# Rotating 96 images: 32 KB load runs, 8 KB store runs and half as many transposes for the middle 64

## The chip, the cores and the metric

The kernel runs on 1 core of one Trainium2 chip. The metric is the device time of one execution in microseconds; lower is better. All runs told of here are fast (granted clock 1.0). "Span" is the part of an execution that the profile covers, from its first to its last instruction. The time is 1.8 us longer than the span in most kernels here, and that difference will matter.

## The reference

```python
def setup_inputs():
    batch, c, h, w = 32, 3, 256, 256
    return {"x": np.random.randn(batch, c, h, w).astype(np.float32)}

def reference(x):
    return np.rot90(x, k=1, axes=(-2, -1)).astype(np.float32)
```

There are 96 images of 256 x 256 float32, 25.17 MB in and 25.17 MB out. No arithmetic is done: every byte is loaded once, moved within the core, and stored once.

## The kernel before

Groups of 16 images (4 MB) pass through an input tile S and an output tile U of 32 KB a partition, three buffers each. The kernel relies on VectorE's transpose to swap partitions and elements within blocks of 32 x 32; the access patterns around it do the rest of the rotation. There are two kinds of group. Kind 1 (first and last 16 images) keeps 8 rows of an image in a partition (8 KB runs in DRAM, transfers of 1 MB). Kind 2 (the middle 64 images) keeps 16 rows (16 KB runs, transfers of 2 MB).

```python
KINDS = [1, 2, 2, 2, 2, 1]
# ... (tile pools S and U, 3 buffers each)
for g, kind in enumerate(KINDS):
    # ...
    if kind == 1:
        R = 8
        # ... (views)
        for s in range(4):                       # 4 loads of 1 MB
            eng = nc.scalar if g == 0 and s % 2 else nc.sync
            eng.dma_start(out=Sv[:, s], in_=xv[s])
        for s in range(4):                       # 4 transposes of 128x2048, 4 stores of 1 MB
            # ... (src and dst patterns)
            nc.vector.transpose(dst, src)
            nc.scalar.dma_start(out=ov[s], in_=Uv[:, s])
    else:
        R = 16
        # ... (views)
        for b in range(2):                       # 2 loads of 2 MB
            nc.sync.dma_start(out=Sv[:, b], in_=xv[b])
        src = Sv.rearrange("p b (r k q) -> p q r k b", r=R, q=R)[:, ::-1, :, ::-1]
        dst = Uv.rearrange("p a (q k r) -> p q r k a", q=R, r=R)
        for q in range(R):                       # 16 transposes of 128x512
            nc.vector.transpose(dst[:, q], src[:, q])
        for a in range(2):                       # 2 stores of 2 MB
            nc.scalar.dma_start(out=ov[a], in_=Uv[:, a])
```

Loads are issued from SyncE (queue 1; two of the first four from ScalarE), stores from ScalarE (queue 10).

## Time and profile before

| | before |
|---|---|
| time, median of the first 3 runs | 124.03 us (123.91 to 124.1) |
| span | 122.2 us |
| VectorE busy | 91.5 us, 75% |
| mean DMA rate | 412 GB/s |
| VectorE's program as built | 89 instructions, 72 of them transposes (the trace records 87) |

The page of the kernel before. In the two rows of slices each digit is the busy share of one fortieth of the span in tenths; the GB/s row has the rate of the same slices. Then the DMA queues (packets, MB, share of 16 engines' time), and VectorE's groups of instructions (busy time, mean ns of one, idle time before).

```profile
span 122.2 us, 172 instructions
DVE 91.5 (75%) x72; POOL 0.2 (0%) x4
...
DVE  0039999729999999996599993199999999548000
...
DMA  4999999999999999999999999999999999999993
GB/s 83 418 426 429 445 343 432 464 424 402 426 469 397 429 434 434 429 429 434 429 440 429 429 434 434 424 418 445 418 432 445 402 453 410 464 426 397 426 429 142
DMA packets 4610, 50.34 MB, mean 412 GB/s; under 512 B 513, under 2 KB 513, under 8 KB 513
...
q10 hardware_dynamic: 2592, 27.26, 52.5%
q1 hardware_dynamic: 2016, 23.07, 45.2%
q14 instruction: 2, 0.01, 0.0%
...
L66 DVE STREAM_TRANSPOSE U<-S 128x512 f32<-128x512 f32 x64 | 60.6, 1050 | 9.8 <-DMA S<-in_x_dram 5.5
L50 DVE STREAM_TRANSPOSE U<-S 128x2048 f32<-128x2048 f32 x8 | 31.0, 3950 | 11.3 <-DMA S<-in_x_dram 11.3
```

What to see: the DMA row is 9 from the second slice to the second to last, VectorE's row is not. The DMA engines bound the kernel.

The timeline of the same kernel (start, length, engine, what, how often, and the wait before it). ACTq and SPq are the issues of transfers.

```profile
1.63 45.47 SPq L61 DMA_DIRECT2D S<-in_x_dram  x8
8.17 15.44 DVE L50 STREAM_TRANSPOSE U<-S 128x2048 f32<-128x2048 f32 x4 [8.17 <-DMA S<-in_x_dram]
...
26.77 30.22 DVE L66 STREAM_TRANSPOSE U<-S 128x512 f32<-128x512 f32 x32 [3.16 <-DMA S<-in_x_dram]
...
59.34 15.20 DVE L66 STREAM_TRANSPOSE U<-S 128x512 f32<-128x512 f32 x16 [2.35 <-DMA S<-in_x_dram]
78.88 15.20 DVE L66 STREAM_TRANSPOSE U<-S 128x512 f32<-128x512 f32 x16 [4.33 <-issue]
...
108.69 3.97 DVE L50 STREAM_TRANSPOSE U<-S 128x2048 f32<-128x2048 f32 x1 [3.15 <-DMA S<-in_x_dram]
```

VectorE takes 15.1 to 15.2 us for 16 images and waits before three of the four middle groups, without the DMA row ever falling: its waits cost nothing.

### The profile page before, as it was taken

The numbers are of one execution on the slowest core, as the hardware profiler recorded it, in microseconds if no ns is written. First come the engines' busy times: TensorE is split into PE (matmuls) and PEld (weight loads), VectorE is DVE, ScalarE is ACT, GpSimd is POOL, SyncE is SP. The second block draws the span as 40 slices with busy tenths as digits, with TensorE's granted clock in tenths as the row PEclk, the third lists the DMA queues.
The fourth block names the chain that finished last, engine by engine and source line by source line (L and its number), as shares of the span: only waits on it lengthen the run. The fifth ranks groups of instructions, "written<-read, shape, count | busy, mean of one in ns | idle before, by whom it ended". The sixth has DMA issues, their size and how long they took to land.

```text
span 122.2 us, 172 instructions
## 1 busy us (share of the span) xinstructions
DVE 91.5 (75%) x72; POOL 0.2 (0%) x4
## 2 busy tenths in 40 slices
DVE  0039999729999999996599993199999999548000
POOL 0000000000000000000000000000000000000000
DMA  4999999999999999999999999999999999999993
GB/s 83 418 426 429 445 343 432 464 424 402 426 469 397 429 434 434 429 429 434 429 440 429 429 434 434 424 418 445 418 432 445 402 453 410 464 426 397 426 429 142
DMA packets 4610, 50.34 MB, mean 412 GB/s; under 512 B 513, under 2 KB 513, under 8 KB 513
## 3 DMA queue, kind: packets, MB, share of 16 engines
q10 hardware_dynamic: 2592, 27.26, 52.5%
q1 hardware_dynamic: 2016, 23.07, 45.2%
q14 instruction: 2, 0.01, 0.0%
HBM read 25.17 MB, written 25.17 MB: 412 GB/s over the span
## 4 chain that ended last, share of the span: by engine, by line
DMA 62%; DVE 27%; SPq 1%; issue 1%; DVEq 0%
DMA S<-in_x_dram 46%; DVE U L66 24%; DMA out_dram<-U 16%; DVE U L50 3%; SPq L45 1%; SPq L61 1%; DVEq L66 0%
## 5 line engine op out<-in xcount | busy, mean ns | idle before, releaser
L66 DVE STREAM_TRANSPOSE U<-S 128x512 f32<-128x512 f32 x64 | 60.6, 1050 | 9.8 <-DMA S<-in_x_dram 5.5
L50 DVE STREAM_TRANSPOSE U<-S 128x2048 f32<-128x2048 f32 x8 | 31.0, 3950 | 11.3 <-DMA S<-in_x_dram 11.3
L83 POOL MEMSET const-uint8-127<- 128x1 uint8 x1 | 0.1, 102 | 0.0
L83 POOL MEMSET const-bfloat16-1.0<- 128x1 bf16 x1 | 0.1, 101 | 0.0
L83 POOL MEMSET const-float32-0.0<- 128x1 f32 x1 | 0.1, 98 | 0.2 <-issue 0.2
L83 POOL MEMSET const-float32-1.0<- 128x1 f32 x1 | 0.1, 98 | 0.0
## 6 DMA issues: line engine op xcount, KB each, us to landing
S<-in_x_dram SPq DMA_DIRECT2D x8, 2048.0 KB, 25.0
out_dram<-U ACTq DMA_DIRECT2D x8, 2048.0 KB, 18.0
out_dram<-U ACTq DMA_DIRECT2D x8, 1024.0 KB, 15.0
S<-in_x_dram SPq DMA_DIRECT2D x6, 1024.0 KB, 26.5
S<-in_x_dram ACTq DMA_DIRECT2D x2, 1024.0 KB, 9.9
```

The source lines that it names most:

```text
L45: eng.dma_start(out=Sv[:, s], in_=xv[s])
L50: nc.vector.transpose(dst, src)
L61: nc.sync.dma_start(out=Sv[:, b], in_=xv[b])
L66: nc.vector.transpose(dst[:, q], src[:, q])
L83: nc = _bacc.Bacc("TRN2", target_bir_lowering=False, num_devices=1)
```

## The change

Intent: for the middle 64 images, load in runs of 32 KB (32 rows a partition) with one transfer of 4 MB per 16 images, and store in runs of 8 KB, also in one transfer. The longer load run lets 8 transposes of 128x1024 do what 16 of 128x512 did. S and U become rings of twelve 8 KB slots, so the capacity is the same; the first and last 16 images are treated as before.

```diff
-    KINDS = [1, 2, 2, 2, 2, 1]
+    R = 8
...
+    AS = [1] * 4 + [4] * 4 + [1] * 4
+    NS = NU = 12
...
+    for i, a in enumerate(AS):
+        s = n % NS
...
+        RI = R * a
+        S = S_all[:, s : s + a].rearrange("p a f -> p (a f)")
+        U = U_all[:, s : s + a]
...
-            for b in range(2):
-                nc.sync.dma_start(out=Sv[:, b], in_=xv[b])
+            eng.dma_start(
+                out=S, in_=xg[n : n + a].rearrange("a (qk f) -> qk a f", f=RI * W)
+            )
...
-            src = Sv.rearrange("p b (r k q) -> p q r k b", r=R, q=R)[:, ::-1, :, ::-1]
-            dst = Uv.rearrange("p a (q k r) -> p q r k a", q=R, r=R)
+        src = S.rearrange("p (r k q) -> p q r k", r=RI, q=R)[:, ::-1, :, ::-1]
+        dst = U.rearrange("p a (q k r) -> p q r k a", q=R, r=RI)
...
             for q in range(R):
                 nc.vector.transpose(dst[:, q], src[:, q])
-            for a in range(2):
-                nc.scalar.dma_start(out=ov[a], in_=Uv[:, a])
...
+            nc.scalar.dma_start(
+                out=og[n : n + a].rearrange("a (p f) -> p a f", p=P), in_=U
+            )
```

More of the change, by code (lines that the diff above doesn't have):

```diff
@@ L20 @@
     P = 128
-    G = 16
-    KINDS = [1, 2, 2, 2, 2, 1]
-    assert len(KINDS) * G == N
-    F = G * H * W // P
-    fp32 = mybir.dt.float32
-    xf = x.rearrange("b c h w -> (b c h w)").rearrange("(g f) -> g f", g=N // G)
-    of = out.rearrange("b c h w -> (b c h w)").rearrange("(g f) -> g f", g=N // G)
-    in_pool = ctx.enter_context(tc.tile_pool(name="in_pool", bufs=3))
-    out_pool = ctx.enter_context(tc.tile_pool(name="out_pool", bufs=3))
-    for g, kind in enumerate(KINDS):
-        S = in_pool.tile([P, F], fp32, name="S")
-        U = out_pool.tile([P, F], fp32, name="U")
-        if kind == 1:
-            R = 8
-            Sv = S.rearrange("p (s f) -> p s f", s=4)
-            Uv = U.rearrange("p (s f) -> p s f", s=4)
-            xv = xf[g].rearrange("(s p f) -> s p f", s=4, p=P)
-            ov = of[g].rearrange("(s p f) -> s p f", s=4, p=P)
-            for s in range(4):
-                eng = nc.scalar if g == 0 and s % 2 else nc.sync
-                eng.dma_start(out=Sv[:, s], in_=xv[s])
-            for s in range(4):
-                src = Sv[:, s].rearrange("p (r k q) -> p q r k", r=R, q=R)[:, ::-1, :, ::-1]
-                dst = Uv[:, s].rearrange("p (q k r) -> p q r k", q=R, r=R)
-                nc.vector.transpose(dst, src)
-                nc.scalar.dma_start(out=ov[s], in_=Uv[:, s])
-        else:
-            R = 16
-            Sv = S.rearrange("p (b f) -> p b f", b=2)
-            Uv = U.rearrange("p (a f) -> p a f", a=2)
-            xv = xf[g].rearrange("(b a qk f) -> b qk a f", b=2, a=2, f=F // 2)
-            ov = of[g].rearrange("(b a qk f) -> a qk b f", b=2, a=2, f=F // 2)
-            for b in range(2):
-                nc.sync.dma_start(out=Sv[:, b], in_=xv[b])
-            src = Sv.rearrange("p b (r k q) -> p q r k b", r=R, q=R)[:, ::-1, :, ::-1]
-            dst = Uv.rearrange("p a (q k r) -> p q r k a", q=R, r=R)
@@ new lines @@
+    R = 8
+    F = R * W
+    G = N // 4
+    AS = [1] * 4 + [4] * 4 + [1] * 4
+    assert sum(AS) == G
+    NS = NU = 12
+    fp32 = mybir.dt.float32
+    xf = x.rearrange("b c h w -> (b c h w)")
+    of = out.rearrange("b c h w -> (b c h w)")
+    xg = xf.rearrange("(n f) -> n f", n=G)
+    og = of.rearrange("(n f) -> n f", n=G)
+    S_all = ctx.enter_context(tc.tile_pool(name="S", bufs=1)).tile([P, NS, F], fp32, name="S_all")
+    U_all = ctx.enter_context(tc.tile_pool(name="U", bufs=1)).tile([P, NU, F], fp32, name="U_all")
@@ new lines @@
+    n = 0
+    for i, a in enumerate(AS):
+        s = n % NS
+        assert s + a <= NS
+        RI = R * a
+        S = S_all[:, s : s + a].rearrange("p a f -> p (a f)")
+        U = U_all[:, s : s + a]
+        eng = nc.scalar if i in (1, 3) else nc.sync
+        if a == 1:
+            eng.dma_start(out=S, in_=xg[n].rearrange("(p f) -> p f", p=P))
+        else:
+            eng.dma_start(
[3 more added lines that the diff above has]
+        dst = U.rearrange("p a (q k r) -> p q r k a", q=R, r=RI)
+        if a == 1:
+            nc.vector.transpose(dst[:, :, :, :, 0], src)
+        else:
@@ L65 @@
             for q in range(R):
                 nc.vector.transpose(dst[:, q], src[:, q])
-            for a in range(2):
-                nc.scalar.dma_start(out=ov[a], in_=Uv[:, a])
+        if a == 1:
+            nc.scalar.dma_start(out=og[n].rearrange("(p f) -> p f", p=P), in_=U[:, 0])
+        else:
+            nc.scalar.dma_start(
+                out=og[n : n + a].rearrange("a (p f) -> p a f", p=P), in_=U
+            )
+        n += a
 _INS = ['x']
```

## The prediction

> **What bounds the kernel now.** The 16 DMA engines. The page's slices show them over 90% busy from the second slice to the second to last, at about 430 GB/s; 50.3 MB move. In the packet records the first data packet starts at 1.74 us, the last ends at 121.06 us, and packets took 119.2 us a DMA engine: no hole. VectorE is busy 75%. The Trainium skill, "DMA: Bandwidth & Descriptors", section "Where 436 GB/s comes from", puts the ceiling of the SBUF ports at 435 GB/s; the trace agrees (424 to 429 GB/s in steady stretches). Only overhead per packet and the ends of the span can be won.
>
> **What the change does, costed.**
> - Packets. 8 KB takes 309 ns, 16 KB 611 ns (medians): 302 ns per 8 KB plus 7 ns a packet; 32 KB would take about 1215 ns (estimate from these). Middle now: 2048 x 611 / 16 = 78.2 us an engine. After: 512 loads of 32 KB and 2048 stores of 8 KB, (512 x 1215 + 2048 x 309) / 16 = 78.4 us. Net +0.2 us: longer loads save what shorter stores lose. If 32 KB runs are cut into 16 KB packets: +0.4 us.
> - Issues. Eight loads of 2 MB become four of 4 MB, stores likewise; an issue takes 0.3 to 0.65 us on queues that run ahead: off the path.
> - Transposes. 64 of 128x512 (0.94 us start to start) become 32 of 128x1024. Between those and the 128x2048 ones (3.86 us) I read 1.9 us each: 15.3 us for 16 images against 15.1. Off the path.
> - Queue shares. The same page, section "Queues, rings and completion order", says each DMA engine takes turns between queues packet by packet. The trace agrees: with 16 KB loads against 8 KB stores (18 to 42 us) the queues moved about equal numbers of packets, 262 to 328 against 106 to 166 GB/s. So 32 KB loads should get about 80% of the rate: loads run ahead, the first group's last store lands at about 62 us instead of 46, and VectorE's third middle group is held until then by its output buffer (59.3 now).
>
> **On the critical path?** Only if both queues run empty. I followed transfers, waits and buffers through with these durations; the same bookkeeping puts the last landing of before at 121.1 us (trace: 121.4) and of after at 121.4, with no hole. The first hole would come if a middle group's transposes took over 18.5 us. The edges do not change.
>
> **Prediction:** 124.2 us, 80% range 123.4 to 125.6; faster 0.02, same 0.92, slower 0.06.
>
> **What would show each step.** Span about 122.4 us; 4096 packets of 8 KB at 309 ns and 512 of 32 KB at about 1215 ns (or 1024 of 16 KB); DMA slices 9 throughout; transposes of 128x1024 near 2.0 us each, VectorE busy 92 us; loads at about 340 GB/s and stores at about 85 while both queues have work; VectorE waiting for stores, not loads, before the third middle group; last store issued around 110 us instead of 112.7, without gain.
>
> **What would make it wrong.** Transposes of the new pattern (source stride 32 B, four destinations 8 KB apart) over 2.3 us each: then holes and 2 to 6 us more. 32 KB packets slow, or unfair across engines, so that one lags. A wait on a reused DMA semaphore that empties both queues, since the last groups' loads wait for stores that land late. Faster by 2% would need over the ports' rate; I see no way.

## The result, and the profile after

| | before | after |
|---|---|---|
| time, median (6 runs each) | 123.97 us | 123.56 us (123.44 to 123.7) |
| ratio, 95% interval | | 0.9965 (0.9953 to 0.9978) |
| span | 122.2 us | 121.8 us |
| VectorE busy | 91.5 us | 94.3 us |
| VectorE's program as built | 89 instructions | 53 instructions |

A ratio is the mean time of one kernel's fast runs over that of the other's of the same rounds, so not quite the ratio of the medians that are quoted. Time and class are as predicted: 123.56 us lies in the range, and the change is within 2%. But the sign of the small difference is not: 0.2 us more was forecast, 0.4 us less was measured, and the interval excludes 1. The experiments are about that 0.6 us, and about whether the steps behind "nothing changes" hold.

The page of the kernel after, the same lines:

```profile
span 121.8 us, 127 instructions
DVE 94.3 (77%) x40; POOL 0.2 (0%) x4
...
DVE  0029999779999999996039999899999999993000
...
DMA  4999989899989998999899999999999999999995
GB/s 86 409 422 428 549 355 441 347 503 430 430 358 503 430 430 361 511 441 430 315 431 430 430 430 420 431 428 425 428 425 428 428 425 430 430 430 428 428 430 213
DMA packets 4992, 50.33 MB, mean 413 GB/s; under 512 B 384, under 2 KB 384, under 8 KB 384
...
q10 hardware_dynamic: 3552, 27.26, 53.2%
q1 hardware_dynamic: 1440, 23.07, 45.0%
HBM read 25.17 MB, written 25.17 MB: 413 GB/s over the span
...
L60 DVE STREAM_TRANSPOSE U_all<-S_all 128x1024 f32<-128x1024 f32 x32 | 63.6, 2073 | 8.1 <-issue 6.2
L57 DVE STREAM_TRANSPOSE U_all<-S_all 128x2048 f32<-128x2048 f32 x8 | 30.8, 3925 | 8.2 <-DMA S_all<-in_x_dram 8.2
```

The 8s in the DMA row are no holes. A packet is booked where it starts, and a 32 KB packet takes 1.2 us of a slice of 3 us: slices of 500 GB/s, more than any long stretch here moved, stand beside slices of 350. Over 18 to 42 us the busy share was 1.01 at 433 GB/s. And queue 14 has no line any more.

The timeline of the kernel after:

```profile
1.63 39.83 SPq L50 DMA_DIRECT2D S_all<-in_x_dram  x4
8.24 15.44 DVE L57 STREAM_TRANSPOSE U_all<-S_all 128x2048 f32<-128x2048 f32 x4 [8.24 <-DMA S_all<-in_x_dram]
...
24.97 31.70 DVE L60 STREAM_TRANSPOSE U_all<-S_all 128x1024 f32<-128x1024 f32 x16 [1.30 <-DMA S_all<-in_x_dram]
...
62.83 15.93 DVE L60 STREAM_TRANSPOSE U_all<-S_all 128x1024 f32<-128x1024 f32 x8 [6.15 <-issue]
79.44 15.93 DVE L60 STREAM_TRANSPOSE U_all<-S_all 128x1024 f32<-128x1024 f32 x8 [0.69 <-DVE U_all L60]
95.27 15.38 DVE L57 STREAM_TRANSPOSE U_all<-S_all 128x2048 f32<-128x2048 f32 x4
```

The third middle group starts at 62.83 us instead of 59.34, after 6.15 us of idle time. The reason named is "issue", which only says that the page found no releaser; the completions in the trace show the last store of the first 16 images landing at 62.74 us (45.84 before). That is the wait for an output buffer that was predicted for 62 us.

The packet records in the trace tell the rest: 4096 packets of 8 KB with a median of 309 ns, 512 of 32 KB with 1213 ns. Between 16 and 40 us both queues started exactly 256 packets: the load queue moved 350 GB/s, the store queue 87. In the kernel before, the same 24 us have 415 and 416 packets, 283 and 142 GB/s.

Where did the 0.4 us come from? The trace records 16 completions for each transfer, taken here as one from each of the 16 DMA engines; it does not name the engine. For the last store, times in us:

```
before: 15 engines from 120.47 to 120.78, the 16th at 121.40
after:  16 engines from 120.54 to 120.98
before, queue 14: one packet of 8192 B at 82.68, 309 ns; the 8 KB packet that
        starts on queue 1 as it ends takes 836 ns instead of 309
after,  queue 14: no such packet inside the span
```

The two runs differ by one late engine. The Trainium skill, "CRC Debugging", section "Comparing the Two Runs", calls queue 14 the sequencers' instruction refill. So the theory to test (F): the 72 transposes of before make an instruction stream that needs one more fetch while the kernel runs; the fetch and the slow packet after it put one DMA engine behind by about 0.6 us; since no engine is ever idle, it cannot catch up, and the end waits for it. The rival (P): the gain is one of the transfers themselves, from sizes, queue shares or their number.

### The profile page after: what moved, and what is told of

It reads as the page before. It is cut to its first block, busy times and chain, and to the rows that moved or that the text cites. A ratio compares the mean times of both kernels' runs of the same rounds, so it can differ in the third digit from the quotient of the medians.

```text
span 121.8 us, 127 instructions
## 1 busy us (share of the span) xinstructions
DVE 94.3 (77%) x40; POOL 0.2 (0%) x4
## 4 chain that ended last, share of the span: by engine, by line
DMA 54%; DVE 35%; DVEq 2%; issue 0%
DMA out_dram<-U_all 47%; DVE U_all L57 25%; DVE U_all L60 10%; DMA S_all<-in_x_dram 6%; DVEq L94 2%
## 5 line engine op out<-in xcount | busy, mean ns | idle before, releaser
L60 DVE STREAM_TRANSPOSE U_all<-S_all 128x1024 f32<-128x1024 f32 x32 | 63.6, 2073 | 8.1 <-issue 6.2
L57 DVE STREAM_TRANSPOSE U_all<-S_all 128x2048 f32<-128x2048 f32 x8 | 30.8, 3925 | 8.2 <-DMA S_all<-in_x_dram 8.2
```

Of the source, the lines that this page charges most:

```text
L57: nc.vector.transpose(dst[:, :, :, :, 0], src)
```

## The experiments

Results were correct unless said otherwise. "Outside" is the mean time less the mean span.

| run | transfers of | VectorE's program | queue 14, 8 KB in the span | span | outside | ratio to before (95%) |
|---|---|---|---|---|---|---|
| before | before | 89 | at 82.7 us | 122.2 | 1.8 | 1 |
| after | after | 53 | none | 121.8 | 1.8 | 0.9965 (0.9953 to 0.9978) |
| 8 transposes in before | before | 57 | none | 121.7 | 2.2 | 0.9996 (0.9983 to 1.0009) |
| 4 transposes in before | before | 41 | none | 121.7 | 1.8 | 0.9956 (0.9944 to 0.9969) |
| the same again | before | 41 | none | 121.6 | 1.8 | 0.9942 (0.9929 to 0.9954) |
| after again, beside it | after | 53 | none | 121.9 | 1.8 | 0.9965 (0.9951 to 0.9978) |
| transposes of after split | after | 85 | at 83.8 us | 122.3 | 1.8 | 1.0012 (1.0000 to 1.0025) |
| after, plus 24 tiny memsets | after | 78 | at 83.9 us | 122.4 | 1.8 | 1.0013 (1.0000 to 1.0027) |
| after, plus 4 tiny memsets | after | 58 | none | 121.8 | 2.2 | 1.0002 (0.9988 to 1.0016) |
| after, 16 KB loads | 16 KB / 8 KB | 55 | none | 122.1 | 1.8 | 0.9993 (0.9979 to 1.0006) |
| all 8 KB | 8 KB / 8 KB | 44 | none | 122.5 | 1.8 | 1.0024 (1.0011 to 1.0037) |

The runs were made on several chips; each ratio is to runs of before from the same rounds. Three runs with extra work for VectorE are told below.

### 1. Before with 8 transposes for 16 images (e1_before_8_wrong)

Transfers, buffers and waits are those of before; only the number and pattern of VectorE's instructions change. The pattern with 8 instructions is a stand-in that does not rotate the images, so the result is wrong.

```diff
-            for q in range(R):
-                nc.vector.transpose(dst[:, q], src[:, q])
+            for q in range(8):
+                nc.vector.transpose(
+                    U.rearrange("p (x q) -> p q x", q=8)[:, q],
+                    S.rearrange("p (x q) -> p q x", q=8)[:, q],
+                )
```

> The kernel before with 8 transposes of 128x1024 per 16 images instead of 16 of 128x512 (a stride-8 pattern, wrong result on purpose); all transfers, their sizes and their waits stay those of before, VectorE's instructions fall from 72 to 40. Theory F (the gain of 0.4 us comes from an 8 KB instruction fetch on queue 14 at 82.7 us that the longer instruction stream of before needs; it delays one DMA engine by 0.7 us and the end waits for that engine): no 8 KB packet of queue 14 inside the span, the last store's 16 completions within 0.5 us, and 123.3 to 123.5 us, ratio about 0.995. Rival P (the gain is of packet sizes, queue shares or fewer transfers): as before, 123.9 to 124.1 us, ratio 0.999 to 1.001.

Measured: 123.86 us, ratio 0.9996. By the time alone, rival P had won. But the profile said F: no packet of queue 14, the last store's completions within 0.45 us, and a mean span of 121.7 us, 0.45 us shorter than before. The gain was there and was lost again outside the span: 2.19 us there instead of 1.78. The trace has no packet of any queue after the span, so it does not show what took the time there. A second guess was needed: with 57 instructions VectorE's stream crosses the same boundary in its last few instructions, at the very end, where the fetch can't overlap anything.

### 2. After with its transposes split (e2_after_split)

```diff
-                nc.vector.transpose(dst[:, q], src[:, q])
+                for h in range(0, RI, 16):
+                    nc.vector.transpose(dst[:, q, h : h + 16], src[:, q, h : h + 16])
```

> The kernel after with each 128x1024 transpose cut into two of 128x512 (correct result), so 72 transposes as before, and every transfer of after. Theory F: the 8 KB packet of queue 14 is back inside the span, one engine completes the last store 0.5 to 0.8 us after the others, 124.0 to 124.3 us (ratio to before 1.000 to 1.003). Rival P: no change from after, 123.4 to 123.7 us, ratio 0.9965.

Measured: 124.1 us, ratio 1.0012, as F expects. The fetch is back (83.78 us, 309 ns, followed on queue 1 by a packet of 844 ns), and one engine completes the last store at 121.40 us, 0.54 us after the other fifteen. The whole gain of the change is gone with the transfers of the change still in place. But VectorE was also busier (96.1 us instead of 94.3), so run 7 below is the cleaner one.

### 3 and 4. The sizes alone (e3_after_16k_loads, e4_all_8k)

```diff
 e3:
-            eng.dma_start(
-                out=S, in_=xg[n : n + a].rearrange("a (qk f) -> qk a f", f=RI * W)
-            )
+            xr = xg[n : n + a].rearrange("a (qk f) -> qk a f", f=RI * W)
+            hf = RI * W // 2
+            for h in range(2):
+                eng.dma_start(
+                    out=S[:, h * hf : (h + 1) * hf], in_=xr[:, :, h * hf : (h + 1) * hf]
+                )
 e4:
-    AS = [1] * 4 + [4] * 4 + [1] * 4
+    AS = [1] * 24
```

> The kernel after with each 4 MB load cut into two of 2 MB with 16 KB runs, stores left at 8 KB; 40 transposes. Packet arithmetic (32 x 1213 ns becomes 64 x 611 ns on each engine): 0.29 us slower than after, so 123.8 to 123.9 us, ratio about 0.999; no 8 KB packet of queue 14 in the span. Load queue's share while both queues have work falls from about 80% to about 67%. If the packet overhead did not count (rival: only the instruction fetch counts), 123.5 to 123.6 us as after.

> Every load and store in 8 KB runs and 1 MB transfers, 24 transposes of 128x2048 in all. Packet arithmetic: 32 x 1213 ns becomes 128 x 309 ns on each engine, 0.74 us slower than after, so 124.2 to 124.4 us, ratio 1.002 to 1.003; 48 more completions a queue of 9 ns are nothing. No 8 KB packet of queue 14. Both queues share evenly. If longer runs gave nothing, 123.5 us.

Measured: 123.86 us and 124.23 us. Against after's ratio of 0.9965 that is 0.28% and 0.59% of 124 us more, 0.35 and 0.73 us; the packet arithmetic said 0.29 and 0.74. Each ratio is known to 0.0013, so these two differences are known to about 0.2 us. Between 16 and 40 us the queues started 415 and 416 packets in the first (283 against 142 GB/s, 67%), and 621 and 622 in the second (212 GB/s each). So run lengths do count, by a few nanoseconds a packet, and the shares follow from turns of one packet. But within that they count as forecast, and they do not hold a gain for 32 KB loads with 8 KB stores over 16 KB for both.

### 5. Before with 4 transposes for 16 images (e5_before_4_wrong)

As experiment 1, with 4 transposes of 128x2048 (`range(4)`, `q=4`); VectorE's program falls to 41 instructions. The result is wrong.

> The kernel before with 4 transposes of 128x2048 per 16 images (stride 4, wrong result on purpose); VectorE's program falls from 89 to 41 instructions, transfers and waits unchanged. The run with 8 (57 instructions) had a span 0.45 us shorter than before, but the time outside the span grew by 0.42 us. Theory F with a boundary (VectorE's instruction stream crosses an 8 KB page at about its 57th instruction plus a fixed tail: with 57 the fetch falls at the very end, where nothing hides it): with 41 no fetch at all, span 121.7, time minus span 1.78, 123.4 to 123.6 us, ratio about 0.996. Rival W (the extra 0.42 us has another cause, as the wrong pattern): time minus span 2.2, 123.8 to 124.0 us.

Measured: 123.46 us, ratio 0.9956, outside 1.80 us. With every transfer of the kernel before unchanged, it is 0.55 us faster, and as fast as after. Rival P falls with this run, and so does the thought that the wrong pattern caused the loss outside the span. The page of this run; it has no queue 14 line:

```profile
span 121.7 us, 124 instructions
...
DMA packets 4608, 50.33 MB, mean 414 GB/s; under 512 B 512, under 2 KB 512, under 8 KB 512
...
q10 hardware_dynamic: 2592, 27.26, 52.6%
q1 hardware_dynamic: 2016, 23.07, 45.6%
```

Against the kernel before, the data queues have the same number of packets and bytes; only the two of queue 14 are missing. The last store completes from 120.53 to 120.88 us, without a late engine.

### 6 and 7. After with tiny instructions added (e6_plus4, e7_plus24)

```diff
+    for k in range(4):        # e7: range(24)
+        nc.vector.memset(U_all[:, 11, k : k + 1], 0.0)
     n = 0
```

One-column memsets, done before the first load lands; the bytes are overwritten before they are stored. Transposes, transfers and waits for transfers are those of after.

> The kernel after plus 4 one-column memsets on VectorE before the first load lands (58 instructions; bytes written are overwritten later, result correct). Boundary theory: the fetch falls at the end: span as after (121.8), time minus span about 2.2 instead of 1.78, 123.9 to 124.0 us, ratio 1.000. Rival (instruction count does not matter): 123.5 to 123.6 us.

> The kernel after plus 24 one-column memsets on VectorE before the first load lands (78 instructions, result correct), transposes and transfers as after. Theory F: an 8 KB packet of queue 14 at about 85 to 95 us, one engine completes the last store 0.4 us or more after the others, span 122.1 to 122.3, time minus span 1.78, 123.9 to 124.2 us, ratio about 1.001. Rival T (in the run with 72 transposes it was their shorter form or longer VectorE time, not the fetch): 123.5 to 123.6 us, no fetch.

Measured: 124.08 and 124.13 us. Both lose the whole gain, each at its own place. With 24 more, the fetch is inside the span (at 83.86 us, a little before the 85 to 95 expected), and the page shows it as the one thing that was added to the queues of after:

```profile
span 122.3 us, 152 instructions
...
DMA packets 4993, 50.34 MB, mean 412 GB/s; under 512 B 384, under 2 KB 384, under 8 KB 384
...
q10 hardware_dynamic: 3552, 27.26, 52.8%
q1 hardware_dynamic: 1440, 23.07, 44.8%
q14 instruction: 1, 0.01, 0.0%
```

4993 packets instead of 4992. Fifteen engines complete the last store by 120.86 us and one at 121.48.

The kept traces let the delay be followed through the run. In e7 no transfer that landed before the fetch had its last engine more than 0.11 us after the fifteenth (e2: 0.07); every store that landed after it had one 0.61 to 0.74 us late (e2: 0.54 to 0.67). So the delay begins with the fetch and is not made up. Its size fits too: the fetch took 0.31 us and the packet behind it 0.53 us more than usual, 0.84 us in all, and the late engine ends 0.75 to 0.86 us after the median engine in the three runs with a fetch. Some trailing occurs without a fetch: two loads of after had one engine 0.55 us late, stores in the middle of before one up to 1.05 us late, and in the repeat of after one engine ended 0.33 us after the others. None of these lasted to the end at the size seen with a fetch. From the first to the last completion of the last store, the runs with a fetch in the span have 0.93 to 1.05 us, those without 0.17 to 0.62.

With 4 more, there is no fetch in the span, which stays at 121.8 us, and the time outside it is 2.21 us. In the three runs with a fetch inside the span (before, e2, e7) VectorE had started 66, 64 and 63 of its recorded instructions (waits included) when it came.

### 8 to 10. How far VectorE is off the path (e8_junk1024, e9_junk2048, e10_junk4096)

A redundant transpose goes ahead of the eight of each 16 images; its output is overwritten.

```diff
+            Uj = U.rearrange("p a f -> p (a f)").rearrange("p (x j) -> p j x", x=1024)   # 2048, 4096
+            Sj = S.rearrange("p (x j) -> p j x", x=1024)
+            nc.vector.transpose(Uj[:, 0], Sj[:, 0])
             for q in range(R):
                 nc.vector.transpose(dst[:, q], src[:, q])
```

> The kernel after with one redundant transpose of 128x1024 ahead of the eight of each 16 images (overwritten, result correct): 17.8 us of VectorE per 16 images instead of 15.8. If VectorE is off the path up to about 18.5 us, as predicted: span within 0.2 us of after's 121.8 and every DMA slice still 9. (56 VectorE instructions: the time outside the span may be 1.8 or 2.2.) Rival: VectorE already bounds part of the run and each 2 us per group costs 2 to 8 us.

> The kernel after with one redundant transpose of 128x2048 ahead of the eight of each 16 images: 19.7 us of VectorE per 16 images. The prediction said that the first hole in the DMA comes beyond about 18.5 us; the same bookkeeping with the measured durations gives 5.1 us more than after here: about 128.7 us (127.5 to 129.5), with slices under 9 in the DMA row in the second half. If VectorE had more slack than that: 123.6 to 124.1 us.

> The same with a redundant transpose of 128x4096: 23.6 us of VectorE per 16 images. Bookkeeping: 20.6 us more than after, about 144.2 us (142.5 to 146), that is, 3.9 us for each of the four middle groups beyond the slack; VectorE busy from the first load on without a wait.

Measured: 123.69, 127.83 and 133.03 us (the last two from two runs each). All three have 56 VectorE instructions and 2.07 us outside the span, so spans are compared. With 17.8 us of VectorE for 16 images the mean span is 121.65 us against after's 121.8: 2 us more of work in each group, 8 us in all, cost nothing. With 19.6 us the span is 125.75, 4.0 us more. There is the hole; the stretches of e9 (length, VectorE busy, POOL busy, granted clock, DMA share, GB/s):

```profile
95.00:98.00 3.00, 3.00 (x3) 0.00 (x0) 1.00 1.02 434
98.00:100.00 2.00, 2.00 (x2) 0.00 (x0) 1.00 0.97 410
100.00:102.00 2.00, 2.00 (x2) 0.00 (x0) 1.00 0.20 82
102.00:104.00 2.00, 2.00 (x2) 0.00 (x0) 1.00 0.00 0
104.00:110.00 6.00, 6.00 (x2) 0.00 (x0) 1.00 0.95 393
```

All loads have landed, the stores of the third middle group are through, and the fourth is still being transposed: nothing is left to move until its store is issued at 103.5 us. The bookkeeping behind the prediction said 5.1 us, for 19.7 us a group; the trace has 4.0.

The third of these runs failed as an experiment; its expectation of 144 us rested on two things that were not so. The 128x4096 transpose was expected to take 7.7 us and took 4.42, and the schedule of the build changed: one transpose of the last 16 images went ahead of the fourth middle group. From the tile view of e10:

```profile
L63 DVE STREAM_TRANSPOSE U_all<-S_all x32: 2066/2084/2119, 29.4 to 109.0; 128x1024 f32<-128x1024 f32 x32
...
L61 DVE STREAM_TRANSPOSE U_all<-S_all x4: 4414/4418/4446, 24.9 to 85.7; 128x4096 f32<-128x4096 f32 x4
```

So its 9 us over after can't be put down to VectorE's time for a group alone, and it is not used.

### 11 and 12. The transfers alone, side by side (e11_after_again, e12_before_4_again)

> The kernel after, unchanged, on the same chip as the next one: 123.5 to 123.6 us, ratio 0.9965.

> The kernel before with 41 VectorE instructions (wrong on purpose) again, beside after: neither fetches inside the span, so what is left between them is the change of transfers alone. Packet arithmetic with the measured 1213 ns: 64 x 611 becomes 32 x 1213 for loads (-0.29 us) and 128 x 309 for stores (+0.45 us), so this one 0.16 us faster than after: 123.4 us, ratio 0.995 to 0.9965. Rival: the new transfers gain something of their own: this one slower than after.

Measured on the same chip: after 123.68 us (0.9965), the transfers of before with 41 VectorE instructions 123.33 us (0.9942). Without the fetch, the old transfers are 0.23% faster, 0.3 us; the first look at the same pair, on different chips, gave 0.0009, 0.1 us. The arithmetic says 0.16; 0.9942 lies just under the 0.995 to 0.9965 expected.

## Why the prediction was right or wrong

**Right: the DMA engines bound the kernel before and after.** No slice has a hole in either, and 8 us of extra work for VectorE did not lengthen the span. The Trainium skill, "DMA: Bandwidth & Descriptors", section "Where 436 GB/s comes from", gives 435 GB/s as the ceiling of the ports; steady stretches after the change ran at 428 to 433. The same section says that for transfers between HBM and SBUF the HBM side, at about 358 GB/s, binds instead; with this kernel on one core the measurement differs: 413 GB/s over the whole span.

**Right: the transfers almost cancel.** Loads went from 64 x 611 ns to 32 x 1213 ns on each engine (-0.29 us), stores from 64 x 611 ns to 128 x 309 ns (+0.45 us). The estimate of 1215 ns for 32 KB was 2 ns off. Without a fetch in either, the new transfers were 0.1 us (different chips) and 0.3 us (same chip) slower than the old ones, about the forecast 0.2, and the two one-sided changes of size gave 0.35 and 0.73 us for 0.29 and 0.74.

**Right: queue shares and the waits that they move.** Forecast: loads about 340 and stores 85 GB/s, the first group's last store landing at about 62 us, the last store issued around 110. Measured: 350 and 87, 62.74, and 110.7.

**Right: VectorE has slack to about 18.5 us for 16 images.** 17.8 us cost nothing, 19.6 us cost 4.0; the runs show no more than that the limit lies between. A transpose of 128x1024 took 2.07 us and came every 1.98 instead of the 1.9 that was read between the two sizes of before. That made 15.9 us for 16 images instead of 15.3, and 94.3 us of busy time instead of 92, within the slack.

**Wrong: the sign of the net.** The prediction was "Net +0.2 us", and of the transposes it said only "64 of 128x512 [...] become 32 of 128x1024 [...] Off the path". As work of VectorE they are off the path. As instructions they are not: the longer stream needed one more fetch, and the sum lacked that term. It measures 0.6 us. Taking the instructions away from before gave 0.55 and 0.7 us (e5, e12); putting 24 memsets into after, and nothing else, cost 0.6 (1.0013 against 0.9965), as did splitting its transposes. Less fetch and more packet overhead make the result: -0.6 for the fetch, as measured on after, and +0.16 by the packet arithmetic are -0.44 us, and -0.43 was measured. (The pairs of e5 and e12, -0.55 with +0.1 and -0.7 with +0.3, must give the same sum: they split the one measured difference.) The time still fell into the range, near its lower edge, since 0.6 us is small beside a range of 2.2. The clue was on the page of before, the line of queue 14, and a packet of 309 ns on one of 16 engines looked like nothing: spread over the engines it is 0.02 us. A second clue was the prediction's own bookkeeping, which put the last landing of before at 121.1 us where the trace has 121.4: fifteen engines had ended by 120.78.

What makes it 0.6 us is that the engines are saturated and the end waits for the last of them. The Trainium skill, "Runtime: NRT & Kernel Launch", section "Instruction fetch mechanics", says of crossing a block boundary that it costs "one DMA tail-bump, mostly hidden". Hidden it was for VectorE, whose transposes started every 0.94 us before, during and after the fetch; on the DMA side the trace does not agree, since one engine, taken to be the one that carried the fetch, finished 0.62 us after the others, in the run with memsets as in before.

**Left open.** Why the packet after the fetch takes 836 to 844 ns instead of 309. And the 0.3 to 0.4 us outside the span with 56 to 58 instructions (five kernels; none with 55 or fewer, none with 78 or more): that it is the same fetch, at the end, fits the order of the counts, but no record shows it. Against it stands that the fetches seen came after 63 to 66 recorded instructions, and these five kernels record only 54 to 56.

**A version that beats both?** 16 KB for loads and stores with few VectorE instructions would (123.33 and 123.46 us), but the two runs that have it give a wrong result, and no run tried an exact pattern with so few. Among correct kernels, after had the lowest ratio (0.9965; e8, with 0.9978, is not clearly apart).

## What to carry to other kernels

In this kernel all 16 DMA engines were busy to the end, and the time was that of the engine that ended last. In such a kernel look at the 16 completions of the last transfer and at everything on the queues, instruction fetches included; here what one fetch added to one engine was never made up. Count instructions as well as their busy time: here merging transposes paid about 0.6 us although VectorE had slack (at least 1.9 us a group, by e8). It paid because it removed one fetch, not for each instruction. And read time and span together: a gain inside the span can be paid back outside it.

## What the Trainium skill lacked or had wrong

- "Runtime: NRT & Kernel Launch", section "Instruction fetch mechanics", gives blocks of 16 KiB (256 instructions) and a mostly hidden cost. Here the fetch inside the span was one packet of 8 KB (whether it was a whole block the trace does not say), it came after 63 to 66 recorded VectorE instructions, and it cost 0.6 us of 124 in a kernel with saturated DMA. No page says that a fetch can delay the data on the engine that carries it.
- "DMA: Bandwidth & Descriptors", section "Queues, rings and completion order", says that engines take turns packet by packet, and gives packets as several descriptors. The runs show a turn for each run of 8, 16 or 32 KB (256 and 256 packets in 24 us), so a queue with longer runs takes the larger share: 350 against 87 GB/s. No page has the time by run length: 309, 611 and 1213 ns.
- "SBUF — State Buffer", section "Door 1: The DMA port swizzle", has a note on 16-byte lines and the need of two accesses to a line. The transposes agree, though only one pattern of that kind was seen: elements 8 bytes apart took 4.42 us for 4096 (1.08 ns each), 16 bytes apart 3.76 us for 2048 (1.84 ns). No page gives the time of a float32 transpose by stride.
- "Runtime: NRT & Kernel Launch", section "The ~15µs preamble/postamble breakdown", lists stages around a kernel, but no page ties the time outside the span to the number of instructions: 1.8 us in most kernels here, 2.07 to 2.2 in the five with 56 to 58 VectorE instructions.
